# A conformer, attention and expert-lookup block on one core: one-hots by pairs of experts, spread loads of y, a fourth landing buffer

## The chip, the core and the metric

The kernel runs on one core of a Trainium2 chip. Its engines work side by side, each through its own queue in order: TensorE (PE) multiplies matrices, VectorE (DVE), ScalarE (ACT) and GpSimd (POOL) do the rest, and SyncE (SP) issues transfers. POOL and ACT issue transfers too, and all transfers share 16 DMA engines. The metric is the device time of one execution in microseconds; the median of the runs counts.

## The reference

One layer over 512 tokens of width 2048. What matters here is its last step, the lookup over 128 x 128 single-neuron experts:

```python
x = x + merged @ w_out[l]
h2 = rms_norm(x, norm2_g[l])
...
q = (ht @ w_query).reshape(T, PEER_HEADS, PEER_QDIM)
idx, gate = peer_route(q, k1, k2)     # 8 heads x 16 experts of 16384 per token, idx = e1 * 128 + e2
...
u = expert_u[ib]
a = jnp.einsum('td,thkd->thk', hb, u)
w = gb.astype(hb.dtype) * jax.nn.gelu(a, approximate=False)
v = expert_v[ib]
return jnp.einsum('thk,thkd->td', w, v)
```

Before it stand a convolution branch, a banded attention branch and their projections.

## The kernel before

Every large product is walked in **tiles of weights** of 1 MB (128 x 4 x 512 floats). A tile is loaded by SP into a `raw` buffer (line 108), split by ACT into a high part `whi` (line 117) and by DVE into a remainder `wlo` (line 118), and multiplied three times by PE (line 153: high by high, high by low, low by high; 48 matmuls of 320 columns a tile in the two products spoken of here). `Net.run` walks the tiles: in step i it issues the load of tile i + 2, splits tile i + 1 and multiplies tile i. Three `raw` buffers (line 104) stand behind the loads, so the load of tile i + 2 waits until tile i - 1 is split.

The expert lookup takes two ways. For 192 of the 512 tokens the rows of `u` and `v` are **gathered** by POOL (line 1138, 1 MB each, into three `gat` buffers, and a fourth in the second product) and multiplied by DVE (line 1165 for `u`; line 1173, `hy`, for `v`). For the other 320 tokens the whole tables are multiplied. The **first product** (128 tiles, `ut`, from 2189 to 3200 us of the span) gives all 16384 activations per token; ACT takes their gelu (`ge`, line 1212) and writes them to HBM (`ged`). The **second product** (128 tiles, `vt`, to the end) multiplies `vt` by activations times gates, and adds to `y`.

The **gates** are placed in a dense matrix by one-hots while the first product runs. `turn` (line 1048) transposes gates and expert numbers so that the 128 chosen experts of a token lie on the partitions: `fe` holds the two halves of each number, `gb` the gate's high part, `ft` its low part. `onehots` (line 1066) makes for 8 tokens three fields of 8 x 128 16-bit values, each by one DVE instruction: two of them compare a row of 0 to 127 (`io128`) with `fe` (line 1074), the third multiplies one by `gb` (line 1077). `scale` (line 1080, ACT) turns one into the low part's field, `place` (line 1086) multiplies the fields on PE (`gps`), ACT copies the result to `sg`, and SP writes `sg` to `g_d` (line 1102) once per 32 tokens. Ahead of that `decode` finds the expert numbers by small compares on DVE, among them one with an operand that is read with step 0 in the innermost place (line 1023, `pb`) and one whose operands all have step 1 there (line 1025, `ib`). One unit (4 tokens) is handed out per tile, 40 calls of `onehots` in all.

The second product opens in `start_m` (line 1236), ahead of the first product's last four tiles. A pool `mp` takes the room of the one-hots and of `sg`; `wload` loads a block of gates (`gt`) and of activations (`gel`) on SP; `wprep` multiplies them (line 1253) and splits the result into `wh` and `wl`. `y` is four tiles of 640 KB, one for each quarter `dc` of the output's width. Each is loaded on POOL when the first tile of its quarter is walked (line 1265), with nothing but the room of its tile to wait for; the first sum into it (line 1274, DVE) stands two tiles later. All walks are written in program order, and a scheduler then sets each engine's order by readiness; `after_split` adds an edge to the last split, as for gathers (`N.after_split(ins, True)`).

Of the kernel before, what the change touches and what calls it, by code (L numbers as in the profile page):

```python
# [23 lines left out]
P = 128  # L24
# [36 lines left out]
class Net:  # L61
    def __init__(self, nc, tc, A):
        self.nc, self.tc, self.A = nc, tc, A
        self.bg, self.late = deque(), deque()
        self.gq = deque()
        self.uq = deque()
        self.gacc, self.grate, self.credit, self.uacc = 0.0, G_E, 0.0, 0.0
        self.subs = []

# [24 lines left out]
    def run(self):  # L94
# [7 lines left out]
        def load(i):  # L102
            src, ncol = self.subs[i][:2]
            raw = self.wp.tile([P, 4, ncol], F32, tag="raw", name="raw", bufs=3)
            for a, b in pieces(i):
                if i == 0:
                    self.beside(a)
                nc.sync.dma_start(raw[:, a:b, :], src[:, a:b, :])
            raws[i] = raw
# [14 lines left out]
        for i in range(n):  # L124
# [6 lines left out]
            while loaded < min(n, i + 3):  # L131
                load(loaded)
                loaded += 1
# [50 lines left out]
def build(nc, tc, A):  # L184
# [806 lines left out]
    def push_route(tt):  # L991
# [56 lines left out]
        def turn():  # L1048
# [4 lines left out]
            fe = rp.tile([P, 2, P], F16, tag="fe", name="fe")  # L1053
            nc.vector.tensor_copy(fe, tr[:, P:3 * P].rearrange("p (j t) -> p j t", j=2))
            g = rp.tile([P, P], F32, tag="gr", name="gr")
            nc.vector.tensor_scalar(g, tr[:, 0:P], GS, None, op0=ALU.mult)
            b = rp.tile([P, P], F16, tag="gb", name="gb")
            lo = rp.tile([P, P], F16, tag="gl", name="gl")
            nc.vector.tensor_copy(b, g)
            nc.vector.tensor_copy(ft, b)  # L1060
# [5 lines left out]
        def onehots(t8):  # L1066

            if "kp" not in S:
# [4 lines left out]
            for w, e in ((1, e2), (0, e1)):  # L1073
                nc.vector.tensor_tensor(e, io128.unsqueeze(1).to_broadcast([P, 8, P]),
                                        R["fe"][:, w, t0:t0 + 8].unsqueeze(2).to_broadcast([P, 8, P]),
                                        op=ALU.is_equal)
            nc.vector.tensor_tensor(hi, e1, R["gh"][:, t0:t0 + 8].unsqueeze(2).to_broadcast([P, 8, P]), op=ALU.mult)
# [157 lines left out]
    def start_m():  # L1235
# [3 lines left out]
        mp = S["mp"] = esM.enter_context(tc.tile_pool(name="mp", bufs=1, side="right"))  # L1239
        wload(0)  # L1240
# [17 lines left out]
    def add_m():  # L1258
        st = {}
        for q in range(16):  # L1260
            for dc in range(4):
                for gg in range(2):
                    def mm(hi, lo, q=q, dc=dc, gg=gg):
                        if gg == 0 and q == 0:
                            nc.gpsimd.dma_start(S["y"][dc], x1_d[dc][:, :, :ND])
# [83 lines left out]
```

## Time and profile before

| | us |
|---|---|
| median of 3 runs | 4121.32 (4121.23 to 4136.25) |
| the profiled execution | 4118.15 |
| its span, first to last instruction | 4116.3 |
| PE busy in the span | 3995.6 |
| DVE busy | 3276.7 |
| ACT busy | 1626.7 |

A busy share is an average over stages with different limits, so the tables by stretch are the ones to read: a stretch where PE is busy all the time is bound by it, and idle time there is lost time. [...] A time line gives in brackets how long the engine had stood before an instruction and what ended that.

### The profile page before, as it was taken

Reading aid. Unit: us, or ns where it says so; the run is one execution under the profiler, and the core shown is the slowest. Engines: PE = TensorE matmul, PEld = TensorE weight load, DVE = VectorE, ACT = ScalarE, POOL = GpSimd, SP = SyncE. Lnnn points to the kernel's source line nnn. Section 1 sums busy time; section 2 is a strip of 40 time slices with the busy share of each in tenths; the row PEclk is TensorE's granted clock in tenths of the full one; section 3 lists DMA queues with packets and bytes.
Section 4 is the critical chain, followed back from the end, with each engine's and each line's share of the span. In section 5 each row is a group of like instructions: output and inputs, shape, how many; then the busy total and the mean of one; then the engine's idle time right before and its main releaser. Section 6 shows DMA issues by size and latency. Waiting matters only on the chain.

```text
span 4116.3 us, 58192 instructions
## 1 busy us (share of the span) xinstructions
PE 3995.6 (97%) x23898; PEld 3769.8 (92%) x23898; DVE 3276.7 (80%) x3969; ACT 1626.7 (40%) x2230; POOL 952.6 (23%) x501
## 2 busy tenths in 40 slices
PE   8999999999999999999999999999998999999999
PEld 6888999999788768999999998899998999999999
DVE  6876777777522589888799999888886989998996
ACT  4211554554432464223323336455554333323332
POOL 0000000000000000244311232344333634444452
PEclk9999999999999999999999999999999999999999
DMA  4322223233433697899857897899999999999996
GB/s 156 105 100 92 100 95 103 93 105 103 160 124 115 245 329 294 312 358 352 329 201 267 329 344 276 305 342 354 349 347 367 394 367 398 383 401 361 389 362 248
DMA packets 228524, 1075.95 MB, mean 261 GB/s; under 512 B 21376, under 2 KB 97216, under 8 KB 120352
## 3 DMA queue, kind: packets, MB, share of 16 engines
q1 hardware_dynamic: 136832, 604.55, 40.3%
q0 software_dynamic: 63776, 434.63, 27.4%
q10 hardware_dynamic: 27648, 33.04, 2.2%
q8 instruction: 187, 3.06, 0.3%
q14 instruction: 81, 0.66, 0.0%
HBM read 1002.87 MB, written 69.21 MB: 260 GB/s over the span
## 4 chain that ended last, share of the span: by engine, by line
PE 70%; DMA 11%; DVE 11%; issue 5%; ACT 2%; POOL 1%; SPq 0%; ACTq 0%; DVEq 0%; POOLq 0%
PE acc L153 66%; DMA gat<-u,ix 4%; DVE wlo L118 4%; DMA raw<-ut 2%; DMA raw<-wfm 2%; DVE gat L1165 2%; ACT whi L117 1%; DMA gat<-v,ix 1%; POOL gat L1138 1%; DMA gel<-ged 1%; DVE hy L1173 1%; PE gps L1095 1%; PE trp L469 0%; DMA sgd<-go 0%; DMA g_d<-sg 0%
## 5 line engine op out<-in xcount | busy, mean ns | idle before, releaser
L117 ACT CAST whi<-raw 128x2048 fp32r<-128x2048 f32 (+2 forms) x515 | 951.3, 1848 | 1909.8 <-PE acc L153 1611.1
L118 DVE TENSOR_TENSOR wlo<-raw,whi 128x2048 fp32r<-128x2048 f32 (+2 forms) x515 | 1136.9, 2208 | 507.1 <-PE acc L153 328.7
L153 PE MATMUL acc<-hah,whi 128*128 128x320 f32 x2048 | 615.5, 314 | 17.0 <-ACT ge L1212 13.6
L153 PE MATMUL acc<-hal,whi 128*128 128x320 f32 x2048 | 607.8, 311 | 0.0
L153 PE MATMUL acc<-wh,whi 128*128 128x320 f32 x2048 | 603.3, 308 | 0.7 <-ACT ge L1212 0.7
L153 PE MATMUL acc<-wl,whi 128*128 128x320 f32 x2048 | 603.2, 310 | 0.0
L1138 POOL DMA_INDIRECT gat<-v,ix x128 | 332.7, 2599 | 525.0 <-DVE wlo L118 459.7
L153 PEld LDWEIGHTS acc<-hah,whi 128*128 128x128 f32 x2048 | 387.2, 189 | 20.0 <-ACT ge L1212 15.9
L153 PEld LDWEIGHTS acc<-hal,whi 128*128 128x128 f32 x2048 | 389.2, 190 | 0.0
L153 PEld LDWEIGHTS acc<-wl,whi 128*128 128x128 f32 x2048 | 386.4, 189 | 0.0
L153 PEld LDWEIGHTS acc<-wh,whi 128*128 128x128 f32 x2048 | 384.6, 188 | 1.0 <-ACT ge L1212 1.0
L361 DVE SCALAR_TENSOR_TENSOR cacc<-upad,vec,cacc 128x512 f32<-128x512 f32 x480 | 358.4, 750 | 10.3
L1138 POOL DMA_INDIRECT gat<-u,ix x128 | 218.7, 1709 | 627.1 <-DVE wlo L118 332.1
L153 PE MATMUL acc<-hh,whi 128*128 128x512 f32 x896 | 354.6, 396 | 3.2 <-ACT ga L603 3.2
L153 PE MATMUL acc<-hl,whi 128*128 128x512 f32 x896 | 357.3, 399 | 0.0
L153 PE MATMUL acc<-hah,wlo 128*128 128x320 f32 x2048 | 329.7, 313 | 20.8 <-DVE wlo L118 20.6
L153 PE MATMUL acc<-whi,hh 128*128 128x384 f32 x1024 | 347.2, 339 | 0.0
L153 PE MATMUL acc<-whi,hl 128*128 128x384 f32 x1024 | 344.1, 336 | 0.0
L1165 DVE SCALAR_TENSOR_TENSOR gat<-gat,xat 128x2048 f32<-128x2048 f32 x128 | 292.1, 2287 | 51.6 <-DMA gat<-u,ix 51.3
L153 PEld LDWEIGHTS acc<-hah,wlo 128*128 128x128 f32 x2048 | 311.0, 191 | 22.5 <-DVE wlo L118 22.5
L1173 DVE SCALAR_TENSOR_TENSOR hy<-gat,wa,hy 128x2048 f32<-128x2048 f32 x128 | 300.4, 2347 | 34.1 <-DMA gat<-v,ix 33.8
L153 PE MATMUL acc<-wh,wlo 128*128 128x320 f32 x2048 | 323.4, 310 | 3.8 <-DVE wlo L118 3.8
(339 smaller groups left out, 6937.1 us busy)
## 6 DMA issues: line engine op xcount, KB each, us to landing
raw<-wfm SPq DMA_DIRECT2D x191, 1024.0 KB
raw<-ut SPq DMA_DIRECT2D x128, 1024.0 KB
raw<-vt SPq DMA_DIRECT2D x128, 1024.0 KB
raw<-wqkv SPq DMA_DIRECT2D x64, 768.0 KB
ged<-ge ACTq DMA_DIRECT2D x128, 160.0 KB
g_d<-sg SPq DMA_DIRECT2D x20, 1024.0 KB
gt<-g_d SPq DMA_DIRECT2D x32, 640.0 KB
gel<-ged SPq DMA_DIRECT2D x32, 640.0 KB
```

The source lines that it names most:

```text
L117: nc.scalar.copy(hi[:, a:b, :], raw[:, a:b, :])
L118: ins = nc.vector.tensor_tensor(lo[:, a:b, :], raw[:, a:b, :], hi[:, a:b, :].bitcast(F32), op=ALU.subtract)
L153: ins = nc.tensor.matmul(out, *((a, w) if swap else (w, a)), **kw)
L361: nc.vector.scalar_tensor_tensor(r["a"], u[:, i:i + W], vcol(V_DW, ch * TAPS + i), r["a"], op0=ALU.mult, op1=ALU.add)
L1095: nc.tensor.matmul(ps[:, i, :], e2[:, c, :], o[:, c, :], start=j == 0, stop=j == 1)
L1138: ins = nc.gpsimd.indirect_dma_start(out=t.rearrange("p a b -> p (a b)"), out_offset=None, in_=A[src], in_offset=bass.IndirectOffsetOnAxis ...
L1165: N.after_split(nc.vector.scalar_tensor_tensor(t, t, 1.0, S["u", who], op0=ALU.mult, op1=ALU.mult, accum_out=a[:, sl:sl + 1]))
L1173: N.after_split(nc.vector.scalar_tensor_tensor(y, t, S["w", who][:, sl:sl + 1], y, op0=ALU.mult, op1=ALU.add))
```

## The change

Three edits. **One-hots:** `fe` and `gb` store each value twice in a row, and the one-hot instructions walk their fields as 8 x 64 x 2 in place of 8 x 128: in the innermost step of two the compared value is read from two neighbours with step 1, where it was read with step 0 before. To make room, two scratch tiles move to buffers that other steps use. **Loads of y:** each load of a quarter of `y` waits for the last split at its place in the walk. **Fourth buffer:** from `start_m` on every fourth tile lands in a `raw` buffer in the pool `mp`, and loads are issued three tiles ahead.

```diff
--- before.py
+++ after.py
@@ -66,6 +66,7 @@
         self.uq = deque()
         self.gacc, self.grate, self.credit, self.uacc = 0.0, G_E, 0.0, 0.0
         self.subs = []
+        self.more = None
 
     def push(self, cost, fn):
         self.bg.append((cost, fn))
@@ -101,7 +102,10 @@
 
         def load(i):
             src, ncol = self.subs[i][:2]
-            raw = self.wp.tile([P, 4, ncol], F32, tag="raw", name="raw", bufs=3)
+            if self.more and i % 4 == 3:
+                raw = self.more()
+            else:
+                raw = self.wp.tile([P, 4, ncol], F32, tag="raw", name="raw", bufs=3)
             for a, b in pieces(i):
                 if i == 0:
                     self.beside(a)
@@ -128,7 +132,7 @@
                 pre()
             if i == 0:
                 split(0)
-            while loaded < min(n, i + 3):
+            while loaded < min(n, i + (4 if self.more else 3)):
                 load(loaded)
                 loaded += 1
             if i + 1 < n:
@@ -1050,31 +1054,36 @@
             for j, t in enumerate((R["g"], R["e", 0], R["e", 1])):
                 nc.tensor.transpose(tr[:, j * P:(j + 1) * P], t.rearrange("p h k -> p (h k)"), ident)
             ft = rp.tile([P, P], F32, tag="ft", name="ft")
-            fe = rp.tile([P, 2, P], F16, tag="fe", name="fe")
-            nc.vector.tensor_copy(fe, tr[:, P:3 * P].rearrange("p (j t) -> p j t", j=2))
-            g = rp.tile([P, P], F32, tag="gr", name="gr")
+            fe = rp.tile([P, 2, P, 2], F16, tag="fe", name="fe")
+            nc.vector.tensor_copy(fe, tr[:, P:3 * P].rearrange("p (j t) -> p j t", j=2).unsqueeze(3)
+                                  .to_broadcast([P, 2, P, 2]))
+            g = gr.tile([P, P], F32, tag="ixf", name="gf")
             nc.vector.tensor_scalar(g, tr[:, 0:P], GS, None, op0=ALU.mult)
-            b = rp.tile([P, P], F16, tag="gb", name="gb")
-            lo = rp.tile([P, P], F16, tag="gl", name="gl")
-            nc.vector.tensor_copy(b, g)
-            nc.vector.tensor_copy(ft, b)
+            b = rp.tile([P, P, 2], F16, tag="gb", name="gb")
+            lo = gr.tile([P, PH, TK], F16, tag="pb", name="gl").rearrange("p h k -> p (h k)")
+            nc.vector.tensor_copy(b, g.unsqueeze(2).to_broadcast([P, P, 2]))
+            nc.vector.tensor_copy(ft, b[:, :, 0])
             nc.vector.tensor_tensor(g, g, ft, op=ALU.subtract)
             nc.vector.tensor_copy(lo, g)
             nc.vector.tensor_copy(ft, lo)
             R["gh"], R["ft"], R["fe"] = b, ft, fe
 
         def onehots(t8):
+
 
             if "kp" not in S:
                 esQ.close()
                 S["kp"] = esK.enter_context(tc.tile_pool(name="kp", bufs=1, side="right"))
             t0 = t8 * 8
             e1, e2, hi = (S["kp"].tile([P, 8, P], F16, tag=nm, name=nm, bufs=2) for nm in ("oe1", "oe2", "ohh"))
-            for w, e in ((1, e2), (0, e1)):
-                nc.vector.tensor_tensor(e, io128.unsqueeze(1).to_broadcast([P, 8, P]),
-                                        R["fe"][:, w, t0:t0 + 8].unsqueeze(2).to_broadcast([P, 8, P]),
+            shape = [P, 8, P // 2, 2]
+            io, v1, v2, vh = (t.rearrange("p (m c) -> p m c" if t is io128 else "p t (m c) -> p t m c", c=2)
+                              for t in (io128, e1, e2, hi))
+            for w, v in ((1, v2), (0, v1)):
+                nc.vector.tensor_tensor(v, io.unsqueeze(1).to_broadcast(shape),
+                                        R["fe"][:, w, t0:t0 + 8, :].unsqueeze(2).to_broadcast(shape),
                                         op=ALU.is_equal)
-            nc.vector.tensor_tensor(hi, e1, R["gh"][:, t0:t0 + 8].unsqueeze(2).to_broadcast([P, 8, P]), op=ALU.mult)
+            nc.vector.tensor_tensor(vh, v1, R["gh"][:, t0:t0 + 8, :].unsqueeze(2).to_broadcast(shape), op=ALU.mult)
             R["oh", t8] = (e2, hi, e1)
 
         def scale(t4):
@@ -1237,6 +1246,7 @@
         esK.close()
         esR.close()
         mp = S["mp"] = esM.enter_context(tc.tile_pool(name="mp", bufs=1, side="right"))
+        N.more = lambda: mp.tile([P, 4, W], F32, tag="raw", name="raw")
         wload(0)
         S["y"] = [mp.tile([P, 4, ND], F32, name=f"y{kk}") for kk in range(KG)]
 
@@ -1262,7 +1272,7 @@
                 for gg in range(2):
                     def mm(hi, lo, q=q, dc=dc, gg=gg):
                         if gg == 0 and q == 0:
-                            nc.gpsimd.dma_start(S["y"][dc], x1_d[dc][:, :, :ND])
+                            N.after_split(nc.gpsimd.dma_start(S["y"][dc], x1_d[dc][:, :, :ND]), True)
                         if gg == 0:
                             n = 3 - dc % 2
                             st["acc"] = [psa.tile([P, W], F32, tag="acc", name="acc", bufs=5) for _ in range(n)]
```

On POOL around the start of the second product, the four loads of `y` (`y_26569` to `y_26572`) stand among the gathers. Before:

```order
L1138 DMA gat<-v,ix 128x2048 x95
L1265 DMA y_26569<-x1d_106 128x4x320
L1138 DMA gat<-v,ix 128x2048
L1265 DMA y_26570<-x1d_107 128x4x320
L1265 DMA y_26571<-x1d_108 128x4x320
L1138 DMA gat<-v,ix 128x2048
L1265 DMA y_26572<-x1d_109 128x4x320
L1138 DMA gat<-v,ix 128x2048 x29
```

and now:

```order
L1147 DMA gat<-v,ix 128x2048 x103
L1275 DMA y_26569<-x1d_106 128x4x320
L1147 DMA gat<-v,ix 128x2048 x3
L1275 DMA y_26570<-x1d_107 128x4x320
L1147 DMA gat<-v,ix 128x2048 x2
L1275 DMA y_26571<-x1d_108 128x4x320
L1147 DMA gat<-v,ix 128x2048 x3
L1275 DMA y_26572<-x1d_109 128x4x320
L1147 DMA gat<-v,ix 128x2048 x15
```

The first load of `y` moved behind eight more gathers, and two or three gathers stand between one load and the next.

On SP at the same place `gt` and `gel` are the gates and activations of one block, `ut` and `vt` the tiles of the first and second product. Before:

```order
L1102 DMA g_d<-sg 128x16x128 x2
L108 DMA raw<-ut 128x2048
L1245 DMA gt<-g_d 128x1280
L1247 DMA gel<-ged_113 128x1280
L108 DMA raw<-ut 128x2048
L1245 DMA gt<-g_d 128x1280
L108 DMA raw<-ut 128x2048
L1247 DMA gel<-ged_114 128x1280
L108 DMA raw<-vt 128x2048
L1245 DMA gt<-g_d 128x1280
L1247 DMA gel<-ged_115 128x1280
L108 DMA raw<-vt 128x2048
```

and now:

```order
L1111 DMA g_d<-sg 128x16x128 x2
L112 DMA raw<-ut 128x2048
L1255 DMA gt<-g_d 128x1280
L1257 DMA gel<-ged_113 128x1280
L112 DMA raw<-ut 128x2048 x2
L1255 DMA gt<-g_d 128x1280
L1257 DMA gel<-ged_114 128x1280
L112 DMA raw<-vt 128x2048 x2
L1255 DMA gt<-g_d 128x1280
L1257 DMA gel<-ged_115 128x1280
```

The last tile of `ut` moved ahead of the second `gt`, and the second tile of `vt` ahead of the third `gt`. VectorE's order around this place is the same in both kernels.

## Rows read from the trace of the kernel before

**Rows 1.** From the page of the profile: its first line, the busy time of each engine (us, share of the span, instructions), and by engine the chain of work that ended last.

```profile
span 4116.3 us, 58192 instructions
...
PE 3995.6 (97%) x23898; PEld 3769.8 (92%) x23898; DVE 3276.7 (80%) x3969; ACT 1626.7 (40%) x2230; POOL 952.6 (23%) x501
...
PE 70%; DMA 11%; DVE 11%; issue 5%; ACT 2%; POOL 1%; SPq 0%; ACTq 0%; DVEq 0%; POOLq 0%
```

**Rows 2.** Table of busy time by stretch, at the start of the second product and in the rest of it: bounds in us from the span's start, length, busy us and instructions of each engine (PE, weight loads, DVE, ACT, POOL), mean granted clock of TensorE (1.00 is 2.4 GHz), mean busy share of the DMA engines, GB/s.

```profile
3160.00:3190.00 30.00, 17.24 (x109) 16.98 (x108) 13.32 (x8) 7.81 (x5) 6.11 (x4) 0.77 1.02 416
...
3220.00:3250.00 30.00, 26.77 (x165) 26.51 (x164) 22.01 (x15) 7.64 (x4) 14.42 (x5) 0.89 0.93 371
3250.00:3900.00 650.00, 649.40 (x4428) 649.14 (x4428) 599.60 (x506) 204.13 (x117) 301.39 (x119) 1.00 0.98 384
```

**Rows 3.** The same table over the last part of the first product.

```profile
2474.00:2560.00 86.00, 80.54 (x584) 75.60 (x583) 84.23 (x109) 58.81 (x117) 17.47 (x9) 0.98 0.73 256
2560.00:2660.00 100.00, 93.08 (x657) 91.72 (x656) 89.23 (x111) 50.58 (x82) 38.58 (x14) 0.97 0.84 305
2660.00:3134.00 474.00, 461.34 (x3361) 453.26 (x3360) 396.97 (x223) 261.06 (x454) 180.74 (x71) 0.99 0.95 349
```

**Rows 4.** VectorE's instructions from 2100 to 3200 us, grouped by line and shape: line, operation, names, shapes, count, busy us and mean ns of one, idle us before them with its releaser.

```profile
L1074 DVE TENSOR_TENSOR oe<-io,fe 128x1024 f16<-128x1024 f16 x80 | 94.5, 1219 | 0.1
L1077 DVE TENSOR_TENSOR ohh<-oe,gb 128x1024 f16<-128x1024 f16 x40 | 48.8, 1219 | 0.0
L1023 DVE TENSOR_TENSOR eq<-pb,io16b 128x256 bf16<-128x256 bf16 x48 | 18.4, 422 | 0.0
...
L1025 DVE TENSOR_TENSOR eq<-eq,ib 128x256 bf16<-128x256 bf16 x48 | 11.9, 285 | 0.0
...
L1054 DVE CAST fe<-trr 128x256 f16<-128x256 f32 x3 | 1.3, 419 | 0.0
```

**Rows 5.** Busy time of DVE in one-hots of line 1077 alone (one of the three of a batch) from 2474 to 2660 us: bounds, length, busy us and count, clock, DMA share, GB/s.

```profile
2474.00:2660.00 186.00, 15.85 (x13) 0.97 0.79 283
```

**Rows 6.** What TensorE waited for from 2474 to 2660 us: engine, line and releaser, us in total, times, longest.

```profile
PE acc L153 <- ACT ge L1212: 6.5, 2, 5.2
PE acc L153 <- DVE wlo L118: 4.8, 2, 3.1
```

**Rows 7.** Time line of VectorE: start in us, length in us, engine, line, operation, output and inputs with shapes, how many were merged, and in brackets the idle time before it and what ended it. The rows show how one tile's split (`wlo`) stands behind them.

```profile
2604.82 2.35 DVE L1074 TENSOR_TENSOR oe<-io,fe 128x1024 f16<-128x1024 f16 x2
...
2609.35 1.22 DVE L1077 TENSOR_TENSOR ohh<-oe,gb 128x1024 f16<-128x1024 f16 x1
2610.48 2.29 DVE L118 TENSOR_TENSOR wlo<-raw,whi 128x2048 fp32r<-128x2048 f32 x1
```

**Rows 8.** Time line of ScalarE, same columns: two of its splits (`whi`) of 1 MB tiles, and what each had waited for.

```profile
2519.64 1.91 ACT L117 CAST whi<-raw 128x2048 fp32r<-128x2048 f32 x1 [3.41 <-DVE e L1026]
...
2583.05 1.91 ACT L117 CAST whi<-raw 128x2048 fp32r<-128x2048 f32 x1 [11.26 <-DMA raw<-ut]
```

**Rows 9.** What TensorE waited for from 2660 to 3134 us, columns as in rows 6.

```profile
PE acc L153 <- ACT ge L1212: 7.1, 5, 3.9
```

**Rows 10.** Time line of GpSimd's queue from 3139 to 3156 us, columns as in rows 7.

```profile
3150.81 0.80 POOL L1265 DMA_DIRECT2D y<-x1d  x1 [11.94 <-DMA g_d<-sg]
3151.92 1.57 POOL L1138 DMA_INDIRECT gat<-v,ix  x1 [0.30 <-issue]
3153.49 1.59 POOL L1265 DMA_DIRECT2D y<-x1d  x2
3155.39 1.00 POOL L1138 DMA_INDIRECT gat<-v,ix  x1 [0.30 <-issue]
```

**Rows 11.** Time line of VectorE from 3141 to 3237 us, columns as in rows 7; the last two `wlo` here split the second last tile of the first product and the second tile of the second product.

```profile
3141.06 2.29 DVE L118 TENSOR_TENSOR wlo<-raw,whi 128x2048 fp32r<-128x2048 f32 x1 [3.00 <-ACT whi L117]
...
3148.10 2.29 DVE L118 TENSOR_TENSOR wlo<-raw,whi 128x2048 fp32r<-128x2048 f32 x1 [2.48 <-ACT whi L117]
...
3165.76 2.35 DVE L1173 SCALAR_TENSOR_TENSOR hy<-gat,wa,hy 128x2048 f32<-128x2048 f32 x1 [5.63 <-DMA gat<-v,ix]
3179.16 2.35 DVE L1173 SCALAR_TENSOR_TENSOR hy<-gat,wa,hy 128x2048 f32<-128x2048 f32 x1 [11.05 <-DMA gat<-v,ix]
...
3184.24 2.28 DVE L118 TENSOR_TENSOR wlo<-raw,whi 128x2048 fp32r<-128x2048 f32 x1
...
3203.88 2.29 DVE L118 TENSOR_TENSOR wlo<-raw,whi 128x2048 fp32r<-128x2048 f32 x1
...
3216.47 1.68 DVE L1274 TENSOR_TENSOR y<-acc,y 128x320 f32<-128x320 f32 x4
...
3236.43 1.49 DVE L1253 TENSOR_TENSOR gel<-gel,gt 128x1280 f32<-128x1280 f32 x1 [7.95 <-DMA gel<-ged]
```

**Rows 12.** Time line of TensorE: the matmuls that follow the longest gap of that stretch.

```profile
3186.58 4.01 PE L153 MATMUL acc<-hah,wlo 128*128 128x320 f32 x16 [12.76 <-DVE wlo L118]
```

**Rows 13.** Time line of SyncE's queue, columns as in rows 7: loads of `gel` and of `raw` around the start of the second product.

```profile
3157.95 0.32 SPq L1247 DMA_DIRECT2D gel<-ged  x1
3160.92 0.33 SPq L108 DMA_DIRECT2D raw<-vt  x1
...
3186.55 0.33 SPq L108 DMA_DIRECT2D raw<-vt  x1
...
3224.04 0.33 SPq L1247 DMA_DIRECT2D gel<-ged  x1
```

## The prediction

> **What bounds the kernel now.** I read the page's busy times and chain first [rows 1]: PE is busy 3995.6 of 4116.3 us and holds 70% of the chain, so only the 121 us in which it idles, and stretches at the lower clock, can be won. Then the tables by stretch, to see where they lie. In the second product from 3250 to 3900 us PE is busy 649.4 of 650.0 us at clock 1.00 [rows 2]: nothing to win there. What the change touches lies before. From 2474 to 2660 us, where one-hots, decoding and gathers meet on DVE, PE idles 5.5 + 6.9 = 12.4 us, and the clock of 0.98 and 0.97 costs 0.02 x 80.5 + 0.03 x 93.1 = 4.4 us more: 16.8 us [rows 3]. DVE is busy 84.2 of 86 us in the first half of that, so it is the engine the others queue behind. From 2660 to 3134 us PE loses 12.7 us of 474, plus some 4 us by a clock of 0.99, while DVE is at 84% and the DMA engines at 0.95 [rows 3]. At the start of the second product PE loses 30.0 - 17.2 = 12.8 us and 0.23 x 17.2 = 4.0 us by the clock from 3160 to 3190, and 3.2 + 0.11 x 26.8 = 6.1 us from 3220 to 3250 [rows 2]. That is 23 us. The sum of these places, 57 us, is the most that the change can bring; the rest of the span is the same work in the same order.
>
> **One-hots.** 120 instructions of 1219 ns are replaced one for one [rows 4]. Whether they get shorter is read from two compares and products of the same size: with one operand at step 0 in the innermost place 256 two-byte elements take 422 ns, with all operands at step 1 285 ns [rows 4]. So 137 ns per 256 elements go, 0.535 ns each, and the new one-hots, 1024 elements with step 1 everywhere, should take 1219 - 548 = 671 ns: 120 x 0.548 = 66 us less DVE work. No row shows an innermost run of only two elements, with a step of 0 above it; the other bound is 1219 ns as now. I take 671, since the innermost step is what differs between the two rows. [...] What is added: `fe` is cast from 256 to 512 elements and `gb` from 128 to 256, three times each; doubling all of a 419 ns cast [rows 4] bounds both at 3 x 0.8 = 2.5 us, ahead of each batch.
>
> What lies on the path is less than 66 us, since DVE is off it where PE is fed. In 2474 to 2660 there are 13 batches of three one-hots [rows 5], 39 x 0.548 = 21 us of relief, more than the 16.8 us that PE loses. PE's waits there are for `wlo`, 4.8 us, and for ACT's `ge`, 6.5 us [rows 6]. A split stands in DVE's queue behind two or three one-hots [rows 7]; ACT's queue stands behind DVE in turn (its cast at 2519.64 waited for a decoding step) [rows 8]. Not all goes: the split at 2583.05 waited 11.3 us for its `raw` tile [rows 8], and a shorter DVE queue frees the buffer only a little earlier. I take 11 of 16.8, with 3 and 15 as bounds. From 2660 to 3134 the largest wait is again for `ge`, 7.1 us in five pieces [rows 9], with DVE idle 77 us there [rows 3]; I take 2 us of some 16, bounds 0 and 8. Behind a faster DVE the gathers come next: each is issued by the last split, so they start earlier and share the DMA engines with `raw` loads; at 0.73 and 0.84 busy [rows 3] there is room for it in the first 186 us and little after.
>
> **Loads of y.** Now the first load holds POOL's queue for 11.9 us until the last write of `g_d` has landed, and the gathers stand behind it: they leave at 3151.92 and 3155.39, with three of the four loads of 640 KB among them [rows 10]. Their users on DVE wait 5.6 and 11.1 us, and the split at 3184.24 stands behind both [rows 11]; PE waits 12.8 us for that split [rows 12]. In the new order eight gathers more go ahead of the first load. These two are then released by the splits at 3141.06 and 3148.10, so at 3143.4 and 3150.4 [rows 11]. A gather took 3165.76 - 3151.92 = 13.8 us to land [rows 10, 11]; they land at 3157 and 3164. What comes last then is the second block's `gel`, issued at 3157.95 [rows 13]. A later one took 3236.43 - 3224.04 = 12.4 us [rows 11, 13], so it lands near 3170.4, and with two steps of 1.5 us and the split's 2.3 us the split ends near 3175.6 in place of 3186.5. PE runs dry at 3186.6 - 12.8 = 3173.8 [rows 12], so about 2 us of the stall stay, and the clock should not fall: 10.9 + 4.0, 15 us won.
>
> Given back: each load of `y` now starts when a split ends and is needed five DVE instructions later. For the first that is 3206.2 to 3216.5 us, 10.3 us [rows 11], less than the 13.8 us of a gather. DVE would wait some 3.5 us or more, four times, with the following splits behind it. PE has a cover: when a tile's sum is due, the next tile is already split (7 us of work) and so is the high part of the one after. With that cover the four loads cost PE between 0 and 14 us; I take 5, as the wait is inside the cover but DVE has only 8% to catch up with [rows 2]. The loss of 6.1 us from 3220 to 3250, behind `gel`'s wait of 8.0 us [rows 11], I leave and add 1 us, since these loads now fall there. Net for the opening: 15 - 5 - 1 = 9 us won, bounds 17 won and 6 lost.
>
> **Fourth buffer.** The second tile of `vt` leaves SP at 3186.55 now, behind a `gt` that waits for DVE [rows 13]; in the new order it stands ahead of that `gt` and leaves with the first, near 3161. Its 1 MB costs 2.5 us at 416 GB/s [rows 2] in front of the third block, and the tile of `ut` that moved ahead of the second `gt` the same; both are loads that are needed anyway. In the steady part there is no idle time to win: 0. Bounds: 2 us either way.
>
> **Sum.** 11 + 2 + 9 + 0 = 22 us. From the profiled execution's 4118.15 us that gives 4096; the median of the runs shown lies 3.2 us above it, so the forecast for the median is 4121.3 - 22 = 4099 us.
>
> **Rivals.**
> *The transfers only move (DMA-bound opening).* From 3160 to 3190 the DMA engines are busy all the time at 416 GB/s [rows 2], and the change removes no byte. If PE cannot open sooner than the bytes arrive, the 9 us are won at one place and lost at the next: 13 us, 4108 us. For it: 2.6 MB of `y` are 6.3 us at that rate, and they are still due within the next eight tiles. Against it: the gap was an order of queues, and gathers can wait. [...]
> [...]
> *Relief spreads.* If the earlier splits free `raw` buffers early enough to end most waits to 3134 us as well, and `y` costs nothing: 14 + 8 + 15 = 37 us, 4084 us. Against it: transfers at 0.95 there.
> *Slower: y late.* If a load of `y` takes what the second gather took, 3179.16 - 3155.39 = 23.8 us [rows 10, 11], it is 13.5 us late; PE's cover gone, four of them are 54 us, less 15 and 13: 26 us, 4147 us. It decides from about 18 us a load, the 10.3 us plus the cover. Against it: that gather had 2 MB of `y` in its queue.
>
> **How the numbers follow.** Chances: forecast 0.46 (4092 to 4106 us), relief spreads 0.24, transfers only move 0.14, one-hots bring nothing 0.10, slower 0.06. Half a per cent, about what can be told from no change here, is 20.6 us: faster means below 4100.7, which takes the second case and two thirds of the first, 0.55; slower means above 4141.9, the last case, 0.06; the rest, 0.39, is no change. The range reaches from 40 us won (15 + 8 + 17), 4082, to 3 us won, 4118, where the opening gains nothing and the one-hots bring their lower bound; outside lie the slower case and the far ends of the others.
>
> **What would show it.** Right: one-hots near 670 ns; PE's idle time from 2474 to 2660 at 3 to 6 us; no wait of `hy` for gathers ahead of the second last split of the first product, and PE's gap there under 3 us; the sum into `y` waiting a few us for its load, PE not. Wrong: one-hots at 1219 ns; the gap of 12.8 us again, behind `gel` or `y`; more than 1 us of PE idle time in the 650 us of the steady part.

## The result and the profile after

The changed kernel takes 4102.62 us (median of six, 4096.88 to 4109.52) beside 4125.78 us for the kernel before (median of six, 4121.23 to 4136.25): ratio 0.9944, 95% interval 0.9926 to 0.9963. Timed again beside other experiments it gave 0.9962 (0.9948 to 0.9976). So 16 to 23 us are won, where the prediction has 22.

The page of the changed kernel, its span, busy times and chain by engine, as in [rows 1]:

```profile
span 4102.5 us, 58203 instructions
...
PE 3997.0 (97%) x23898; PEld 3771.4 (92%) x23898; DVE 3218.0 (78%) x3969; ACT 1624.0 (40%) x2230; POOL 886.8 (22%) x501
...
PE 73%; DVE 10%; DMA 9%; issue 5%; ACT 2%; POOL 1%; ACTq 0%; SPq 0%; DVEq 0%; POOLq 0%
```

DVE is 59 us less busy, POOL 66 us. What makes DVE's part is in the instructions that write the one-hots `oe` and `ohh` (duration in ns: least, median, most); below the dots stands how long, and how many times, ScalarE's scaling of `oe` waited for them. The second block is that last row in the kernel before:

```profile
L1083 DVE TENSOR_TENSOR oe<-io,fe x80: 671/685/693, 2479.2 to 3094.4; 128x1024 f16<-128x1024 f16 x80
L1086 DVE TENSOR_TENSOR ohh<-oe,gb x40: 641/685/690, 2481.0 to 3097.3; 128x1024 f16<-128x1024 f16 x40
...
  ACT oe L1093: 7.4, 6
```

```profile
  ACT oe L1084: 48.0, 24
```

685 ns in place of 1219 [rows 4] is 120 x 0.534 = 64 us less. ScalarE, which scales the one-hots, waited for them 24 times and 48.0 us before, and 6 times and 7.4 us now.

The three windows of the routing's stage, as in [rows 3], and TensorE's waits in the first two and in the third, as in [rows 6, 9] (us in total, times, longest):

```profile
2474.00:2560.00 86.00, 84.28 (x627) 80.43 (x626) 79.76 (x129) 59.52 (x119) 17.86 (x11) 1.00 0.82 290
2560.00:2660.00 100.00, 92.81 (x652) 91.33 (x651) 83.51 (x107) 51.48 (x85) 26.38 (x13) 0.95 0.85 308
2660.00:3134.00 474.00, 468.81 (x3436) 462.65 (x3436) 360.44 (x224) 260.65 (x451) 137.52 (x73) 0.99 0.96 355
```

```profile
PE acc L157 <- ACT whi L121: 5.6, 1, 5.6
PE acc L157 <- ACT ge L1221: 2.4, 2, 1.6
PE gps L1104 <- DVE ohh L1086: 0.7, 1, 0.7
...
PE acc L157 <- ACT ge L1221: 3.8, 1, 3.8
PE acc L157 <- ACT whi L121: 1.3, 1, 1.3
```

TensorE does not wait for VectorE's splits `wlo` any more (4.8 us in the first 186 us before [rows 6]). One wait of 5.6 us for a high part `whi` is new as a wait of TensorE: ScalarE's cast stood behind a late load. Counted in matmuls started, the three windows have 627 + 652 + 3436 = 4715, against 584 + 657 + 3361 = 4602 before [rows 3].

At the opening of the second product, TensorE's rows with an idle time, then ScalarE, then VectorE, in order of time (start, duration, in brackets the idle time before it and what ended it):

```profile
3164.01 4.16 PE L157 MATMUL acc<-hah,wlo 128*128 128x320 f32 x16 [2.04 <-DVE wlo L122]
...
3179.92 0.41 PE L157 MATMUL acc<-wh,whi 128*128 128x320 f32 x1 [3.54 <-ACT ge L1221]
```

```profile
3176.47 1.26 ACT L246 CAST wh<-gel 128x1280 fp32r<-128x1280 f32 x1 [10.54 <-DVE gel L1263]
3177.64 1.89 ACT L121 CAST whi<-raw 128x2048 fp32r<-128x2048 f32 x1
3179.44 0.75 ACT L1221 ACTIVATE ge<-acc 128x320 f32<-128x320 f32 x2
```

```profile
3148.45 4.73 DVE L1182 SCALAR_TENSOR_TENSOR hy<-gat,wa,hy 128x2048 f32<-128x2048 f32 x2
...
3174.95 1.49 DVE L1263 TENSOR_TENSOR gel<-gel,gt 128x1280 f32<-128x1280 f32 x1 [2.86 <-DMA gel<-ged]
...
3245.91 1.68 DVE L1284 TENSOR_TENSOR y<-acc,y 128x320 f32<-128x320 f32 x4 [2.46 <-DMA y<-x1d]
```

The 12.76 us of [rows 12] are 2.04 us. The uses of the gathers, `hy`, that waited 5.6 and 11.1 us [rows 11] wait for nothing at 3148.45. One sum into `y` waits for its load, 2.46 us, and TensorE not for the sum. But a new wait is there at 3179.92. Read upward: TensorE waits for an `acc` buffer that ScalarE's `ge` reads; `ge` stands on ScalarE behind the cast of the third block's gates, `wh`, which waited 10.54 us for VectorE's product `gel`; that product waited for its load.

To see what is won and given back, the time is cut at the first matmul of the first product (its activations are `hah`) and at the first of the second (`wh`); in the rows of TensorE on these tiles it is the first start. The changed kernel, then the kernel before:

```profile
L157 PE MATMUL acc<-hah,whi x2048: 305/308/636, 2193.8 to 3172.4; 128*128 128x320 f32 x187
L157 PE MATMUL acc<-wh,whi x2048: 307/308/468, 3175.0 to 4089.8; 128*128 128x320 f32 x187
```

```profile
L153 PE MATMUL acc<-hah,whi x2048: 303/308/636, 2188.7 to 3194.8; 128*128 128x320 f32 x187
L153 PE MATMUL acc<-wh,whi x2048: 307/308/468, 3197.5 to 4104.0; 128*128 128x320 f32 x187
```

First product: 3197.5 - 2188.7 = 1008.8 us before, 3175.0 - 2193.8 = 981.2 after, 27.6 won. Second, to the end of the span: 918.8 before, 927.5 after, 8.7 given back.

### The profile page after: what moved, and what is told of

It is laid out like the page before. It is cut to its first block, busy times and chain, and to the rows that moved or that the text cites. A ratio compares the mean times of both kernels' runs of the same rounds, so it can differ in the third digit from the quotient of the medians.

```text
span 4102.5 us, 58203 instructions
## 1 busy us (share of the span) xinstructions
PE 3997.0 (97%) x23898; PEld 3771.4 (92%) x23898; DVE 3218.0 (78%) x3969; ACT 1624.0 (40%) x2230; POOL 886.8 (22%) x501
## 4 chain that ended last, share of the span: by engine, by line
PE 73%; DVE 10%; DMA 9%; issue 5%; ACT 2%; POOL 1%; ACTq 0%; SPq 0%; DVEq 0%; POOLq 0%
PE acc L157 70%; DVE wlo L122 4%; DMA gat<-u,ix 2%; DMA raw<-wfm 2%; DVE gat L1174 1%; DMA gel<-ged 1%; ACT whi L121 1%; DMA gat<-v,ix 1%; PE gps L1104 1%; DVE hy L1182 1%; POOL gat L1147 1%; DMA raw<-ut 1%; PE trp L473 0%; DMA sgd<-go 0%; DVE y L1284 0%
## 5 line engine op out<-in xcount | busy, mean ns | idle before, releaser
L157 PE MATMUL acc<-hah,whi 128*128 128x320 f32 x2048 | 615.0, 314 | 13.2 <-ACT whi L121 6.9
L1147 POOL DMA_INDIRECT gat<-v,ix x128 | 267.2, 2087 | 558.5 <-DVE wlo L122 498.9
L157 PEld LDWEIGHTS acc<-wh,wlo 128*128 128x128 f32 x2048 | 308.3, 190 | 7.8 <-DVE wlo L122 7.8
## 6 DMA issues: line engine op xcount, KB each, us to landing
g_d<-sg SPq DMA_DIRECT2D x20, 1024.0 KB, 13.4
```

What stands on the lines that cost most here:

```text
L157: ins = nc.tensor.matmul(out, *((a, w) if swap else (w, a)), **kw)
L1147: ins = nc.gpsimd.indirect_dma_start(out=t.rearrange("p a b -> p (a b)"), out_offset=None, in_=A[src], in_offset=bass.IndirectOffsetOnAxis ...
```

## The experiments

Every kernel below was cut at the same two matmuls. All times in us; the stages come from one profiled execution, the median and the ratio to the kernel before from 6 to 12 runs. The kernel before ran again in each set: its median was 4125.78 beside the first timing of the changed kernel, 4125.06 beside the first runs of the one-hots alone, `y` alone, buffer alone, and one-hots and `y`, 4127.38 beside `y` and buffer, no `y`, `y` late and gates by ScalarE, and 4123.70 beside the three others. So ratios compare across sets better than medians.

| kernel | first product starts | first | second | both | median | ratio (95%) |
|---|---|---|---|---|---|---|
| before | 2188.7 | 1008.8 | 918.8 | 1927.6 | 4125.78 | |
| before, again | 2193.6 | 1008.9 | 925.3 | 1934.2 | 4129.55 (one run) | |
| one-hots alone | 2195.6 | 995.6 | 923.7 | 1919.3 | 4106.78 | 0.9953 (0.9937 to 0.9969) |
| one-hots alone, again | 2186.9 | 994.5 | 922.2 | 1916.7 | 4107.52 | 0.9969 (0.9957 to 0.9980) |
| y alone | 2198.3 | 994.8 | 930.9 | 1925.7 | 4120.62 | 0.9988 (0.9974 to 1.0002) |
| buffer alone | 2189.7 | 1005.1 | 921.1 | 1926.2 | 4121.65 | 1.0000 (0.9985 to 1.0016) |
| y and buffer | 2195.6 | 998.5 | 928.6 | 1927.1 | 4123.33 | 0.9990 (0.9977 to 1.0004) |
| one-hots and y | 2197.5 | 984.3 | 928.4 | 1912.7 | 4105.34 | 0.9952 (0.9935 to 0.9969) |
| after | 2193.8 | 981.2 | 927.5 | 1908.7 | 4102.62 | 0.9944 (0.9926 to 0.9963) |
| after, again | 2194.6 | 983.0 | 931.8 | 1914.8 | 4111.67 | 0.9962 (0.9948 to 0.9976) |
| after, one-hots twice | 2193.7 | 991.6 | 929.8 | 1921.4 | 4124.24 | 1.0003 (0.9994 to 1.0013) |
| after, no y | 2194.6 | 982.5 | 927.6 | 1910.1 | 4105.49 | 0.9939 (0.9920 to 0.9959) |
| after, y late | 2193.0 | 972.4 | 930.2 | 1902.6 | 4105.00 | 0.9946 (0.9927 to 0.9966) |
| after, gates by ScalarE | 2194.8 | 987.7 | 930.1 | 1917.8 | 4108.29 | 0.9948 (0.9929 to 0.9967) |

How far one profile can be trusted: in the three pairs of one kernel the first product agrees within 2 us and the second within 7. But the kernel with `y` late gives every engine the changed kernel's order of instructions up to 20 us before the second product, and its first product is 9 to 11 us shorter, 972.4 beside 981.2 and 983.0. So two executions of equal work can lie 10 us apart, and a difference of a few us between two single profiles shows little. The start of the first product moves over 11 us, though no edit changes an instruction ahead of it.

One difference stands clear of that. In the five profiles with the loads of `y` as before (before, one-hots alone, buffer alone; stall of 12 to 14 us) the second product takes 918.8 to 925.3 us. In the nine where they are spread, late or gone it takes 927.5 to 931.8.

### One part at a time

**One-hots alone**: the kernel before with

```diff
-            fe = rp.tile([P, 2, P], F16, tag="fe", name="fe")
...
+            fe = rp.tile([P, 2, P, 2], F16, tag="fe", name="fe")
...
-                nc.vector.tensor_tensor(e, io128.unsqueeze(1).to_broadcast([P, 8, P]),
...
+                nc.vector.tensor_tensor(v, io.unsqueeze(1).to_broadcast(shape),
```

and the rest of that part. Expected:

> The kernel before with the pairs of one-hots alone. Theory (the terms of the prediction add up): the 120 one-hot operations take about 685 ns each, TensorE's gaps between the routing's start and the end of the first product shrink from about 25 us to about 14, the 12.8-us stall at the opening of the second product stays at 11 to 13; ratio about 0.997, some 11 to 13 us faster. Rival (the relief of VectorE also frees the opening, since the gathers' products come earlier): the stall falls under 6 us and the whole gain of the change, 20 us or more, is there already. Rival (one-hots bring nothing): within 3 us of before.

Measured: ratio 0.9953, some 19 us, which lies between theory and rival; but the stall stayed:

```profile
3180.31 4.00 PE L153 MATMUL acc<-hah,wlo 128*128 128x320 f32 x16 [13.16 <-DVE wlo L118]
```

So the first rival falls by its mechanism: the relief does not open the second product, and yet this part alone has most of the gain. The profiled execution lay 10 us above its own median, so the kernel was run again.

> The kernel before with the pairs of one-hots alone, once more, since its first profiled execution lay 10 us above its own median. If the one-hots alone carry the gain: ratio to before near 0.9955, first and second product together 8 to 18 us shorter than in the kernel before, although the stall at the opening is still 11 to 14 us. If the first timing was chance: ratio 0.997 or above.

Ratio 0.9969, just short of the 0.997 that would have meant chance; stall 11.94 us. The two intervals overlap only from 0.9957 to 0.9969; taken together some 16 us (19 and 13). By stages the first product is 13 to 14 us shorter and the second not.

**y alone** (`N.after_split(nc.gpsimd.dma_start(S["y"][dc], ...), True)` in place of the plain issue). Expected:

> The kernel before with the loads of y spread over the tiles alone. Theory: the stall ahead of the first split of the second product falls from 12.8 us to 2 to 4, the gaps in 2474 to 3134 stay at about 25 us, and the second product gives some 5 us back; ratio about 0.998, 6 to 10 us faster. Rival (transfers only move): the stall goes but as much comes back within 100 us as waits for weights and gates, within 3 us of before. Rival (not additive): the stall stays over 8 us, because without the fourth landing buffer the gates' products still come late.

The first product is 14.0 us shorter, 1008.8 to 994.8; the second 5.6 to 12.1 longer than in the two profiles of before. Ratio 0.9988, some 5 us, with an interval that holds no change: between the theory's 6 to 10 us and the rival's 3. The stall fell to 4.47 us, now a wait for a high part `whi`. Of the 14.0 us won in the first product 5.6 to 12.1 are given back, nearer to the rival than to the theory.

**Buffer alone** (`N.more` and the load four ahead). Expected:

> The kernel before with the fourth landing buffer of the second product alone. Theory: the stall stays at 11 to 13 us, since it is VectorE that is late there and not the weights; within 3 us of before. Rival (the buffer does the work at the opening): the stall falls under 6 us, ratio 0.998 or less. Rival (one more 1-MB load ahead in the crowded opening takes bandwidth from y and the gates): the stall grows by 2 to 5 us, ratio 1.001.

```profile
3183.61 3.84 PE L157 MATMUL acc<-hah,wlo 128*128 128x320 f32 x13 [13.26 <-DVE wlo L122]
```

The stall is there in full, the ratio 1.0000. Theory held, within the 6 us either way that the interval (0.9985 to 1.0016) leaves.

**One-hots and y**, the changed kernel without `N.more`. Expected:

> The changed kernel without the fourth landing buffer. Theory: within 2 us of the changed kernel, ratio to before about 0.9945; in the second product TensorE's waits for weights are as long as in the changed kernel, 6 to 10 us in all. Rival (the fourth load ahead is what crowds the opening and gives the 9 us back): the second product is 3 to 8 us shorter than the 927.5 us of the changed kernel, and this kernel is faster than it. Rival (the buffer earns its keep): 3 us or more slower than the changed kernel, with TensorE waiting for weights in the steady part.

Ratio 0.9952, second product 928.4 as in the changed kernel's two profiles (927.5, 931.8). The fourth load ahead neither crowds the opening nor helps it.

**y and buffer**, the changed kernel with the one-hots of before. Expected:

> The changed kernel with the one-hots of before (single-value walk). Theory (the one-hots bring 8 to 18 of the 23 us, by VectorE being early in the routing's stage): gaps of 22 to 25 us in that stage again, ratio to before about 0.998. Rival (the opening carries the gain, one-hots add little once y is spread): ratio 0.996 or less.

Ratio 0.9990. In the three windows of [rows 3] its TensorE is busy 635.8 of 660 us, as before (635.0; 645.9 in the changed kernel). Theory held: without the pairs no gain is left that the timing can tell.

**The one-hots twice.** To tell VectorE's time from anything else that the new form brings:

```diff
-            for w, v in ((1, v2), (0, v1)):
+            for w, v in ((1, v2), (1, v2), (0, v1), (0, v1)):
...
-            nc.vector.tensor_tensor(vh, v1, R["gh"][:, t0:t0 + 8, :].unsqueeze(2).to_broadcast(shape), op=ALU.mult)
+            for _ in range(2):
+                nc.vector.tensor_tensor(vh, v1, R["gh"][:, t0:t0 + 8, :].unsqueeze(2).to_broadcast(shape), op=ALU.mult)
```

> The changed kernel with each of the 120 paired one-hot operations issued twice in a row, so that VectorE spends 2 x 685 ns where before it spent 1219. Theory (the gain is VectorE's time in the routing's stage and nothing else of the pairs): the gain of the one-hots goes; TensorE's gaps from 2474 to the end of the routing are 20 us or more, time within 5 us of the changed kernel with the one-hots of before, ratio to before 0.998 to 1.002. Rival (it is the walk in pairs itself, or the storage that moves with it, that helps, by the gathers or the transfers): ratio stays at 0.996 or less.

Ratio 1.0003 (0.9994 to 1.0013): the gain of the whole change is gone, with `y` spread and the fourth buffer in place. ScalarE's wait for the one-hots, and the first two windows of [rows 3]:

```profile
  ACT oe L1094: 49.2, 24
```

```profile
2474.00:2560.00 86.00, 79.96 (x586) 75.25 (x586) 84.34 (x138) 53.94 (x106) 17.36 (x10) 1.00 0.74 263
2560.00:2660.00 100.00, 92.51 (x636) 89.87 (x635) 92.69 (x131) 51.33 (x85) 29.77 (x14) 0.95 0.84 304
```

VectorE is busy 84 us of the first 86 again, and TensorE starts 586 matmuls in them (584 before, 627 in the changed kernel). It is VectorE's time that counts, not the storage or the walk, which are those of the changed kernel here. (Twice 685 ns is 12% more than the 1219 ns of before, so the run overshoots a little.) In the first 186 us theory held by its sign; of the expected 20 us of gaps this profile has 13.5 us to 2660 and only some 5 from there to 3134, and its span of 4115.1 us lies below the median too, so for the time the many runs count.

### What the second product gives back

**No y.** The loads go, and the first sums are copies:

```diff
-                            N.after_split(nc.gpsimd.dma_start(S["y"][dc], x1_d[dc][:, :, :ND]), True)
...
+                            if q == 0:
+                                nc.vector.tensor_copy(y, st["acc"][dt][:, :ND])
```

> The changed kernel without the loads of y: the first sums are copied instead of added to the residual, which is left out. Theory A (the 2.6 MB of y in the crowded opening are what the second product gives back): TensorE's waits in the first 200 us of the second product fall from 9.2 us to 4 or less, the second product takes 919 to 922 us in place of 927.5, and the kernel is 5 to 9 us faster than the changed one, ratio to before about 0.993. Theory B (the give-back comes from the gates' and activations' own loads, which were hidden by the stall before): the second product stays at 925 or more, within 3 us of the changed kernel.

**y late.** The residual is loaded in the last 16th, into the buffers of the gates, and added there:

```diff
+                            N.after_split(nc.vector.tensor_tensor(y, y, wts["x", dc], op=ALU.add))
...
+                            nc.sync.dma_start(wts["x", x], x1_d[x][:, :, :ND])
```

> The changed kernel with the residual loaded at the end of the second product (in its last 16th, into the buffers of the gates) and added there by VectorE; the first sums are copied. Theory A: the opening as without y, nothing given back at the end, where VectorE has idle time; 4 to 8 us faster than the changed kernel. Theory B: within 3 us of it. Rival (the late load and four more additions of VectorE make its last sums late): the last 60 us take 2 to 5 us longer, and nothing is won.

Theory A asked, without `y`, for waits of 4 us or less in the first 200 us of the second product and for a second product of 919 to 922 us. Both signs fail, and with `y` late as well. The second product takes 927.6 and 930.2 us, as with the loads. The times alone could not tell: the interval without `y`, 0.9920 to 0.9959, holds theory A's 0.993 as well as the changed kernel's 0.9944. In the second kernel the last 60 us are as busy as the changed kernel's (TensorE 53.7 and 53.5 us), so its late additions cost nothing; its short first product comes before anything that was edited. TensorE's waits in those 200 us (us in total, times, longest), in the changed kernel and then without `y`:

```profile
PE acc L157 <- DVE wlo L122: 5.6, 4, 2.4
PE acc L157 <- ACT ge L1221: 3.5, 1, 3.5
```

```profile
PE acc L157 <- ACT ge L1221: 5.5, 1, 5.5
PE acc L157 <- DVE wlo L122: 3.7, 3, 1.7
```

The sums are 9.1 and 9.2 us (13.4 with `y` late), but not at the same places. Without `y` two waits for splits are gone, 2.02 us at 3222.47 and 2.43 at 3282.98; the wait for `ge` is 2 us longer, and the splits from 3338 to 3443 cost 6.0 us where they cost 2.1. So the loads of `y` do cost TensorE some 4.5 us, and without them as much comes back elsewhere. The DMA engines have as little room without them: 1.02 and 419 GB/s in the first 30 us, 1.00 and 399 in the next, beside 1.02 and 416, 1.01 and 410 with them, so other transfers take the place. Whether all these bytes together bind the opening, no run here separates.

The new wait for `ge` is there in both, with 5.50 and 6.00 us. TensorE and ScalarE without `y`:

```profile
3183.95 0.64 PE L157 MATMUL acc<-wh,whi 128*128 128x320 f32 x1 [5.50 <-ACT ge L1221]
```

```profile
3180.50 1.26 ACT L246 CAST wh<-gel 128x1280 fp32r<-128x1280 f32 x1 [10.85 <-DVE gel L1263]
```

It is the same chain as in the changed kernel: load of `gel`, product, cast, and `ge` behind the cast. In the kernel before TensorE's wait at this place was

```profile
3199.55 0.42 PE L153 MATMUL acc<-wh,whi 128*128 128x320 f32 x1 [0.75 <-ACT ge L1212]
```

From the first matmul of the second product to the first of its third tile the kernel before took 15.1 us and the changed kernel 19.4, in the second profiles 15.2 and 22.4. So this place holds 4.3 of the 8.7 us that the second product is longer in the first pair of profiles, and 7.2 of 6.5 in the second. Yet the chain is not the whole of it. With the gates' writes issued by ScalarE (last experiment below) a stall of 9.29 us hides it again, TensorE waits 0.65 us for `ge`, and the second product takes 930.1 us all the same, 5.72 of them in a wait for a split at 3229.

SyncE's issues of the second and third block's `gel` in the changed kernel, and what SyncE waited for ahead of the third block's `gt` and `gel`:

```profile
3146.36 0.33 SPq L1257 DMA_DIRECT2D gel<-ged  x1
...
3161.78 0.33 SPq L1257 DMA_DIRECT2D gel<-ged  x1
```

```profile
SPq L1255 <- DVE gel L1263: 5.6, 1, 5.6
...
SPq L1257 <- DVE wl L247: 1.0, 1, 1.0
```

Gates and activations share three buffers (`gg`), two to a block. The third block's `gt` leaves at 3160.38, as the second block's product (3158.86 to 3160.35) ends; its `gel` leaves at 3161.78, as the split `wl` of the first block (3160.27 to 3161.75) ends. The product with it starts at 3174.95, 13.2 us later, with the DMA engines full (first row below). So the ring holds the issue back; how much of the wait is the ring's and how much the 13 us of the load is not shown, for a fourth buffer was not tried. The stretches from 3160 to the second product and 60 us into it, in the changed kernel and in the kernel before:

```profile
3160.00:3175.00 15.00, 12.96 (x78) 12.70 (x77) 12.14 (x8) 4.96 (x3) 5.61 (x2) 0.89 1.02 425
3175.00:3235.00 60.00, 54.44 (x349) 53.92 (x348) 51.15 (x35) 20.18 (x15) 24.57 (x12) 0.94 1.01 413
```

```profile
3160.00:3197.00 37.00, 24.24 (x156) 23.98 (x155) 20.32 (x12) 8.72 (x6) 12.81 (x5) 0.82 1.02 415
3197.00:3257.00 60.00, 56.02 (x362) 55.50 (x361) 51.46 (x36) 19.30 (x15) 30.31 (x11) 0.94 0.97 388
```

### A wait left in the first product

The 5.6 us before 2592.32 seem to come from loads of `raw` that stand on SyncE's queue behind two writes of gates. **Gates by ScalarE**: `nc.scalar.dma_start(g_d..., sg)` in place of `nc.sync.dma_start`. Expected:

> The changed kernel with the writes of the gates issued from the queue of ScalarE, which makes them, in place of SyncE's, where they wait ahead of the loads of weights. Theory (the 5.6-us gap at 2592 and the 1.4 and 3.9 at 2690 come from loads that stand behind a waiting write): these gaps fall under 2 us each, the first product is 6 to 10 us shorter, ratio to before about 0.9925. Rival (bandwidth makes the loads late, not the order): the gaps stay, within 3 us of the changed kernel. Rival (ScalarE pays for the issues and the splits come later): 2 us or more slower.

Ratio 0.9948, no gain; the first product is 4.7 to 6.5 us longer than in the changed kernel's two profiles, not 6 to 10 shorter. SyncE in the changed kernel, then ScalarE here:

```profile
2564.18 13.32 SPq L1111 DMA_DIRECT2D g_d<-sg  x2
2577.60 17.34 SPq L112 DMA_DIRECT2D raw<-ut  x4
```

```profile
2562.87 12.92 ACTq L1111 DMA_DIRECT2D g_d<-sg  x2
2575.91 3.71 ACT L121 CAST whi<-raw 128x2048 fp32r<-128x2048 f32 x2 [12.57 <-issue]
```

ScalarE itself had just filled `sg`, and the profile shows nothing that this issue waited for. Still the second of the two writes of 1 MB held its queue for 12.4 us (the first took 0.38), as it held SyncE's for 12.5, and the casts to `whi` now stand behind it. The gaps of 5.6 and 1.6 us there became 1.3, 2.2 and 2.7, and others came: 3.7 us at 2736, and 9.29 us at the opening. The casts there wait for no load any more (7.29 us at 2590.37 in the changed kernel, none at 2587.18 here), so order it was and not bandwidth. Part of the gain went back by the second rival's mechanism: the wait changed its queue. The 9.29 us stand behind the second block's product, which waited 9.94 us for its load; what made that load late is not shown.

## Why the prediction was right

**One-hots, price of one.** 671 ns forecast, 685 measured, by the run of two that no row had shown. Right.

**One-hots, worth.** 11 + 2 = 13 us forecast. Kernels that differ in the one-hots alone: first product 1008.9 to 995.1 (means of two), 998.5 to 982.1 (mean of two), 994.8 to 984.3, so 13.8, 16.4 and 10.5 us, mean 13.6; the second product does not change by more than 3. The times say 16. The sum was right, its split was not. From 2474 to 2660 TensorE's idle time fell from 12.4 to 8.9 us (7 to 9 in the other kernels with the pairs), not to 3 to 6, and the clock gave nothing back: 4.4 us by the prediction's reckoning before, 0.05 x 92.8 = 4.6 now. So the term of 11 us measured some 3 there. The prediction let 5.8 of 16.8 us stay, and 13.5 stayed, 5.6 of them a wait for a late `raw`, which it had feared of [rows 8]. More came later: in the third window TensorE's busy time went from 461.3 to 468.8 us, 7.5 us where the term had 2; in the second profile of either kernel it is 464.6 and 466.5, so 2 to 7.5. All three windows hold 7.6 to 10.9 us; where the rest of the 13.6 lies is not shown.

**The stall.** 2 us forecast to stay of 12.8, 2.04 measured; "no `hy` wait", "a gap under 3 us" and "a sum into `y` that waits a few us, PE not" held as put. As a mechanism this step was right: the 2.04 us stand behind the second block's `gel`, as forecast. The 4 us for the clock came in part: from the stall to the first 60 us of the second product the granted clock was 0.82 over 37 us and 0.94 over 60 before, 0.89 over 15 us and 0.94 over 60 now: 37 x 0.18 = 6.7 us became 15 x 0.11 = 1.7, and the second stretch loses its 3.6 as before. The lower level itself shows in the stall of the kernel before: granted clock 1.00 from 3160 to 3175 us, 0.50 from 3180 to 3189 and 1.00 again from 3192 to 3202; no run shows either level in GHz.

**What the opening is worth.** Here a term was mis-sized. 15 us won and 6 given back, net 9, was the forecast. The edit to `y` alone won 14.0 us in the first product and lost at least 5.6 in the second; over the three pairs that differ by it, first product 14.0, 6.6 and 10.8 us shorter, second 8.9, 7.5 and 5.5 longer (means where there are two profiles): 10.5 won, 7.3 lost, net 3. The times agree: 0.9988 and 0.9990 with their intervals on both sides of 1, and in the one set with both kernels the changed one (4111.67), expected 2 to 6 us faster than the one-hots alone, was not faster (4107.52). So the opening is worth about 3 us by the stages, most of them single profiles, and the times can't tell that from nothing.

**Who gives it back.** The prediction put 5 of the 6 us to `y` loads that come late for their sums. That step failed: VectorE waited for one such load, 2.46 us, inside TensorE's cover, and without any `y` load in the opening the second product is as long. What the runs showed in its place is waits that move. The stall had hidden the chain of the third block of gates, which the prediction left out: TensorE's wait behind it grew from 0.75 to 3.54 us (6.59 in the second profile). The loads of `y` cost two splits some 4.5 us, but without them other waits grew as much; and where a stall of 9.29 us hid the chain again, a split cost 5.72 us instead. The rival "the transfers only move" was nearest for this part: the opening's gain was won at one place and mostly lost at the next. It had the bytes of `y` for its reason, and without those nothing was won; whether the bytes of all transfers are the reason, with the DMA engines full in every case looked at, stays open.

**Fourth buffer.** 0 forecast, ratio 1.0000 alone (0.9985 to 1.0016) and no difference that the timing can tell on top of the other two. Right as far as it can be told.

**The rivals.** "The one-hots bring nothing" fell: they are nearly all. "Relief spreads" fell as a sum: 37 us are not there, and a load that stands behind another queue's work keeps its wait. "Slower: y late" fell: one load came 2.5 us late, where 13.5 would have been needed. One sign of being wrong did appear: from 3250 to 3900 TensorE is idle 4.5 us, not 1 or less (0.6 before). It separates little, for the second profile of the kernel before has 4.0 there. The changed kernel's row, as in [rows 2]:

```profile
3250.00:3900.00 650.00, 645.51 (x4386) 644.46 (x4385) 595.83 (x501) 199.78 (x114) 299.84 (x117) 1.00 0.97 382
```

So the forecast of 22 us met 16 to 23 with a term for the one-hots that was 1 to 3 us small and one for the opening that was some 6 us large. Errors of opposite sign did part of the work, within the one-hots' term too: that the total came out so near was in part luck.

## What to carry to other kernels

Count what a stall hides before putting a price on its removal: here 12.8 us of waiting for one queue lay over other waits that were nearly as late, and by the stages 7 of 10 us came back behind it. Shortening the work of the engine that is busy 98% of a stage was worth more here (13 to 19 us) than a better order of queues (some 3), and doubling the shortened work is a quick test of whether it is that engine's time. Before an issue is moved to another queue, look how long it holds the one it is on: here the hold moved with it.

## What had not been expected

**An issue that takes 13 us.** The writes of `g_d`, 1 MB each, go out in pairs. The first of a pair took 0.4 to 0.6 us to issue, the second 1.7 to 12.5 us over the ten pairs of the changed kernel (SyncE) and 1.8 to 12.4 us where ScalarE issues them, there with its data ready. Loads of 1 MB went out in 0.3 us when nothing was in their way. The view of waits puts the longest hold on SyncE down to ScalarE's cast `whi` (12.3 us), and the one on ScalarE to nothing. Why the second is held is not shown.

**POOL's gathers and the walk.** The time in which POOL issues one gather from `v` (ns: least, median, most); the kernel before, the changed kernel, and the one-hots twice:

```profile
L1138 POOL DMA_INDIRECT gat<-v,ix x128: 935/2322/7280, 2458.0 to 3328.2; - x128
```

```profile
L1147 POOL DMA_INDIRECT gat<-v,ix x128: 933/1850/6210, 2462.8 to 3313.2; - x128
```

```profile
L1148 POOL DMA_INDIRECT gat<-v,ix x128: 932/1378/7417, 2463.4 to 3326.4; - x128
```

The medians scatter: 2082 to 2322 ns in five profiles with the one-hots of before, 1620 to 2080 in eight with the pairs. The sum is clearer. In the three windows of [rows 3] POOL is busy 236.8 us in the kernel before (217 to 237 in those five), 181.8 in the changed kernel (179 to 194 in those eight) and again 181.8 with the paired one-hots twice. So POOL's busy time goes with the length or the form of VectorE's single instruction, not with VectorE's load (in these windows VectorE is busy 570.4 us in the kernel before, 523.7 in the changed kernel and 585.4 with the one-hots twice). How the one acts on the other is not shown, and no run here separates length from form. It was worth nothing in time that could be told: the kernel with the one-hots twice is as slow as the one before.

**How far equal work can drift.** The start of the first product lay between 2186.9 and 2198.3 us in kernels that do not differ before it. Differences of less than 10 us between two single spans say nothing here. Cut at two of its own matmuls the same work repeats better, within 2 us in the three pairs, but not always: the first product of the kernel with `y` late shows 10 us.
